# Forgetting attention on one core: the second group of transposed probabilities moves to the unit's own second PSUM bank

## The chip, the cores and the metric

The kernel runs on one core of a Trainium2 chip. The metric is the device time of one execution in microseconds (us). Three executions of the kernel before took 2426.31, 2428.12 and 2430.02 us; their median, 2428.12 us, is the time before.

## The reference

The reference is a two-layer trunk on a sequence of 1024 tokens of width 1024. Layer 0 mixes tokens with forgetting attention, layer 1 with a diagonal state-space mixer; each is followed by a SwiGLU block, and each of the four blocks has a norm before and after it. The change lies in the attention of layer 0, 16 heads of 64 columns:

```
for blk in range(seq_len // Q_BLOCK):          # 8 blocks of 128 queries
    s = einsum(qb, kb) * scale                 # against all keys up to the block's end
    s = s + c[q] - c[k]                        # sums of log forget gates
    s = where(q_pos >= k_pos, s, -inf)
    p = softmax(s)
    outs.append(einsum(p, vb))
o = concatenate(outs) * sigmoid(gate)
return o @ w_out
```

## The kernel before

Matrix products in full precision are made of two or three products of rounded parts: each operand is split into a high part, which ScalarE rounds to, and a low part, which VectorE gets by subtraction. So every operand that TensorE has made itself goes through a ScalarE copy and a VectorE subtraction that both read PSUM.

PSUM has eight banks of 512 float32 columns per partition, and the kernel holds all of it as one tile, `ps`, of which it hands out regions by hand. In the attention stage banks 0 and 1, and banks 2 and 3, are two slots of two banks for the scores, which alternate from unit to unit (`S`); banks 4 and 5 are for the projections (`PROJ`), bank 6 is for the transposes (`PTB`), bank 7 for the products with the values (`PVB`). Waits on PSUM are kept bank by bank.

`attend` runs over units, a unit being one head and one block of 128 queries; in each head the blocks go from 7 down to 0, and block `qb` sees `(qb + 1) * 128` keys. A unit passes three steps:

- `scores` (L542): TensorE makes the scores in the slot's banks (L551 and L552, one pair of matmuls for each 512 keys). Blocks 4 to 7 need both banks, blocks 0 to 3 the first alone. VectorE adds the bias in place and takes the row's minimum (L555). ScalarE writes the exponentials to SBUF, in `Pt`, with the row's sum (L561); `Pt` has two buffers. In the last two heads VectorE and GpSimd also divide by the sum (L563, L564).
- `transposes` (L576), one unit later: TensorE transposes the exponentials, 128 by 128, in groups of up to four which fill one bank (L588). ScalarE copies the group as the high part (L591), VectorE subtracts for the low part (L592). Blocks 4 to 7 have two groups, blocks 0 to 3 one; that makes 12 groups in a head, 192 in all.
- `values` (L594), for two units at a time, up to three units later: TensorE multiplies with the values in bank 7 (L607), and ScalarE and VectorE add the two halves into `o` (L611, L612).

Next to the attention of one pair of heads run the projections of the next pair and the gate of the pair before (`qkv`, `gate`; their matmuls are L272, L273, L274). `weave` writes the streams into one program in proportion to given weights, a chunk at a time (12 matmuls for a projection); the `yield` lines in `attend` tell it how much TensorE work has been written. The framework then places instructions on each engine's queue: it keeps the order of the program as a priority, and puts a later instruction first where, by its own times, an earlier one isn't ready. On the chip each engine's queue runs in the order so fixed. So projection matmuls stand between the transposes of one unit, at places that the planner chose. After the last head, the output projection (`out_proj`, L674) takes the scores' slots in the same turn.

The lines around the change:

```
units = [(h, qb) for h in range(NH) for qb in reversed(range(8))]
ps = self.S("S")                      # in scores: the slot of this unit
p2 = self.pb(PTB, (P, 4, P))          # in transposes: bank 6, for each group
nc.tensor.transpose(p2[:, i], p[:, (g + i) * P:(g + i + 1) * P], self.ident)
nc.scalar.copy(dh, p2[:, 0:n])
nc.vector.tensor_sub(dl, p2[:, 0:n], f32(dh))
```

Of the kernel before, what the change touches and what calls it, by code (L numbers as in the profile page):

```python
# [14 lines left out]
P = 128  # L15
# [16 lines left out]
PTB = (2,)  # L32
# [3 lines left out]
def f32(ap):  # L36
    return ap.bitcast(F32)
# [121 lines left out]
class Trunk:  # L159
# [369 lines left out]
    def attend(self, c, o):  # L529

        nc = self.nc
        units = [(h, qb) for h in range(NH) for qb in reversed(range(8))]
        An, pt, Pt, pv, rs, ri = {}, {}, {}, {}, {}, {}

        def load_bias(h):
            An[h] = self.R("An")
            nc.sync.dma_start(An[h], self.bcast(self.csum[h:h + 1, :], D))  # L540

        def scores(h, qb):  # L542
            qh, ql = c[h // 2]["q"][h % 2 * 2:h % 2 * 2 + 2]
            k = c[h // 2]["k"][h % 2]
            nk = (qb + 1) * P
            qs = slice(qb * P, nk)
            nc.gpsimd.tensor_add(An[h][:, qs], An[h][:, qs], self.cmask)  # L547
            ps = self.S("S")
            for c0 in range(0, nk, 512):
                c1 = min(c0 + 512, nk)  # L550
                nc.tensor.matmul(ps[:, c0:c1], qh[:, qs], k[:, c0:c1], start=True, stop=False)  # L551
                nc.tensor.matmul(ps[:, c0:c1], ql[:, qs], k[:, c0:c1], start=False, stop=True)  # L552
            with self.tc.high_priority(AHEAD):
                m = self.small("mx")
                nc.vector.tensor_tensor_reduce(out=ps[:, :nk], in0=ps[:, :nk], in1=An[h][:, :nk], op0=ALU.add, op1=ALU.min,  # L555
                                               scale=1.0, scalar=3e38, accum_out=m)
            p = Pt[h, qb] = self.R("Pt")
            if h // 2 not in rs:
                rs[h // 2] = self.small("rs", (P, 2, 8))
            r = rs[h // 2][:, h % 2, qb:qb + 1]  # L560
            nc.scalar.activation(p[:, :nk], ps[:, :nk], AF.Exp, bias=m, scale=-1.0, accum_out=r)  # L561
            if h >= NH - 2:
                nc.vector.reciprocal(r, r)  # L563
                nc.gpsimd.tensor_scalar(p[:, :nk], p[:, :nk], r, 1.0, op0=ALU.mult, op1=ALU.mult)  # L564

        def sums(hp):

            p2, r, x = self.pb(PTB, (P, P))[0:16], self.small("ri", (16, P)), self.R("RI")
            nc.tensor.transpose(p2, rs.pop(hp).rearrange("p a b -> p (a b)"), self.ident)
            nc.vector.reciprocal(r, p2)  # L570
            nc.sync.dma_start(self.ri_d[hp], r)
            for i in range(2):
                nc.sync.dma_start(x[i * 64:i * 64 + 64], self.bcast(self.ri_d[hp][i * 8:i * 8 + 8], D, 64))
            ri[hp] = x

        def transposes(h, qb):  # L576
            j, qq = qb // 2, qb % 2
            if qq:
                ng = (2 * j + 2 + 3) // 4
                pt[h, j] = [(self.R("pth", (P, 4, 256), F32R), self.R("ptl", (P, 4, 256), F32R)) for _ in range(ng)]  # L580
            p = Pt.pop((h, qb))
            for g in range(0, qb + 1, 4):
                n = min(4, qb + 1 - g)
                if g:
                    yield 0.11 * 4
                p2 = self.pb(PTB, (P, 4, P))
                for i in range(n):
                    nc.tensor.transpose(p2[:, i], p[:, (g + i) * P:(g + i + 1) * P], self.ident)  # L588
                th, tl = pt[h, j][g // 4]
                dh, dl = th[:, 0:n, qq * P:qq * P + P], tl[:, 0:n, qq * P:qq * P + P]  # L590
                nc.scalar.copy(dh, p2[:, 0:n])  # L591
                nc.vector.tensor_sub(dl, p2[:, 0:n], f32(dh))  # L592

        def values(h, j):  # L594
            h2, vt = h % 2, c[h // 2]["v"]
            if h2 == 0 and j == 3:
                o[h // 2] = self.R("o")
            r = slice(h2 * 64, h2 * 64 + 64)
            if j % 2:
                pv[h] = self.pb(PVB)  # L600
            out = pv[h][:, (j % 2) * 256:(j % 2) * 256 + 256]
            last = 2 * j + 1
            t = pt.pop((h, j))
            seq = [(0, 0)] + [(kb, i) for kb in range(1, last + 1) for i in (0, 1)] + [(0, 1)]
            for n, (kb, i) in enumerate(seq):
                lo = P if kb == last else 0
                nc.tensor.matmul(out[:, lo:], vt[kb // 4][:, kb % 4, h2, :], t[kb // 4][i][:, kb % 4, lo:],  # L607
                                 start=(n == 0), stop=(n == len(seq) - 1))
            if j % 2 == 0:
                d = o[h // 2][r, (j // 2) * 512:(j // 2) * 512 + 512]  # L610
                nc.scalar.copy(d, pv[h][64 - h2 * 64:128 - h2 * 64])  # L611
                nc.vector.tensor_add(d, d, pv[h][r])  # L612
                if h2 and j == 0 and h < NH - 2:
                    nc.gpsimd.tensor_mul(o[h // 2], o[h // 2], ri.pop(h // 2))

        load_bias(0)
        for i in range(len(units) + 3):
            hp = min(i, len(units) - 1) // 16
            if i < len(units):
                h, qb = units[i]  # L620
                if qb == 7:
                    yield 0.0, hp
                scores(h, qb)
                if qb == 2 and h + 1 < NH:
                    load_bias(h + 1)
                yield 0.16 * (qb + 1), hp
            if 1 <= i <= len(units):
                h, qb = units[i - 1]
                for x in transposes(h, qb):
                    yield x, hp  # L630
                yield 0.11 * (qb % 4 + 1), hp
                if h % 2 and qb == 0 and h < NH - 2:
                    sums(h // 2)
            if i >= 3 and (i - 3) % 2 == 1:
                h, qb = units[i - 3]
                values(h, qb // 2)
                yield 0.22 * (qb + 1), hp
# [1066 lines left out]
```

## Time and profile before

| what | before |
|---|---|
| median of three runs | 2428.12 us |
| profiled execution | 2426.33 us |
| its span | 2424.5 us |
| granted TensorE clock | 0.995 |
| TensorE matmul busy | 2359.3 us (97%) |
| VectorE busy | 1689.1 us (70%) |
| ScalarE busy | 1204.4 us (50%) |
| transposes, L588, attention stage | 576 matmuls, 100.2 us |
| ScalarE copies of them, L591 | 192, 92.0 us |
| VectorE subtractions, L592 | 192, 106.4 us |

The profile tells one execution. Its time is 1.8 us under the median. A busy time is the sum of an engine's records; matmuls are pipelined, and the end of a matmul's record is modelled, so that records overlap and a waiting TensorE loses more than the idle time between records. "PEld" is the load of weights, which runs under the matmuls. In rows of the timeline the first number is the start in us from the start of the span, the second the length; in brackets stands the engine's idle time before the row and what ended it. The attention stage lies between about 72 and 672 us.

### The profile page before, as it was taken

How to read it: one execution, taken by the hardware profiler on the slowest of the kernel's cores; microseconds unless marked ns; L12 is line 12 of the kernel's file. 1: busy time of each engine (PE TensorE's matmuls, PEld its weight loads, DVE VectorE, ACT ScalarE, POOL GpSimd, SP SyncE). 2: the span in 40 equal slices, each digit the busy share in tenths (PEclk: the TensorE clock that was granted, in tenths of full speed). 3: DMA queues.
4: the chain of work that ended last, by engine and by line, in shares of the span. 5: the costliest groups of instructions: out<-in, count | busy, mean ns of one | idle time of the engine just before them, and what ended most of it. 6: DMA issues, size and time to landing. Idle time of an engine off the chain costs nothing.

```text
span 2424.5 us, 31559 instructions
## 1 busy us (share of the span) xinstructions
PE 2359.3 (97%) x11683; PEld 1938.8 (80%) x11683; DVE 1689.1 (70%) x2684; ACT 1204.4 (50%) x2029; POOL 455.2 (19%) x427
## 2 busy tenths in 40 slices
PE   7999999999999999999999999999999999999997
PEld 5777778777777888888878779888878888888886
DVE  6867776677678967666668686763795656555867
ACT  6766676667646333434564563232453333333334
POOL 4222222222400034545520001410000000000003
PEclk9999999999999999999999999999999999999999
DMA  4121112121243444343688752443424333237874
GB/s 146 48 61 53 49 48 62 53 61 54 87 149 101 121 127 135 117 136 116 204 293 301 270 170 84 135 147 107 135 80 135 107 98 109 92 118 261 284 239 157
DMA packets 252427, 318.23 MB, mean 131 GB/s; under 512 B 34225, under 2 KB 179937, under 8 KB 252273
## 3 DMA queue, kind: packets, MB, share of 16 engines
q1 hardware_dynamic: 252272, 316.23, 40.9%
q8 instruction: 91, 1.49, 0.3%
q14 instruction: 64, 0.52, 0.1%
HBM read 238.46 MB, written 77.72 MB: 130 GB/s over the span
## 4 chain that ended last, share of the span: by engine, by line
PE 74%; DVE 12%; ACT 7%; DMA 3%; issue 3%; POOL 0%; SPq 0%; DVEq 0%; ACTq 0%; POOLq 0%
PE ps L841 33%; PE ps L943 10%; PE ps L272 7%; PE ps L274 7%; PE ps L273 7%; PE ps L588 2%; PE ps L607 2%; DVE ps L555 1%; DMA raw<-in_ffn_w_down_dram 1%; DMA rot_d<-ry 1%; ACT wh L253 1%; PE ps L552 1%; PE ps L551 1%; DVE ptl L592 1%; DVE y L318 1%
## 5 line engine op out<-in xcount | busy, mean ns | idle before, releaser
L841 PE MATMUL ps<-B,ah 128*128 128x512 f32 x1056 | 326.0, 390 | 0.3 <-ACT B L89 0.3
L943 PE MATMUL ps<-wdh,gh 128*128 128x512 f32 x616 | 241.4, 392 | 6.3 <-ACT m L962 3.7
L943 PE MATMUL ps<-wdh,gl 128*128 128x512 f32 x616 | 240.9, 391 | 1.9 <-DVE gl L254 1.9
L943 PE MATMUL ps<-wdl,gh 128*128 128x512 f32 x616 | 240.9, 391 | 0.8 <-DVE wdl L254 0.8
L841 PEld LDWEIGHTS ps<-B,ah 128*128 128x128 f32 x1056 | 198.1, 188 | 42.7 <-ACT B L89 1.2
L841 PE MATMUL ps<-ops,ah 128*128 128x512 f32 x704 | 218.2, 391 | 0.0
L272 PE MATMUL ps<-hT,wh 128*128 128x512 f32 x512 | 207.5, 406 | 1.3 <-DVE pt L429 0.7
L841 PE MATMUL ps<-B,al 128*128 128x512 f32 x528 | 205.4, 389 | 0.0
L273 PE MATMUL ps<-hT,wh 128*128 128x512 f32 x512 | 204.4, 399 | 0.0
L274 PE MATMUL ps<-hT,wl 128*128 128x512 f32 x512 | 202.6, 396 | 0.0
L253 ACT CAST gh<-gr 128x1024 fp32r<-128x1024 f32 (+1 forms) x78 | 81.1, 1040 | 166.4 <-PE ps L943 138.0
L592 DVE TENSOR_TENSOR ptl<-ps,pth 128x512 fp32r<-128x512 f32 x192 | 106.4, 554 | 78.6 <-ACT pth L591 73.6
L254 DVE TENSOR_TENSOR gl<-gr,gh 128x1024 fp32r<-128x1024 f32 (+1 forms) x78 | 98.3, 1262 | 84.0 <-ACT gh L253 83.7
L841 PEld LDWEIGHTS ps<-ops,ah 128*128 128x128 f32 x704 | 131.5, 188 | 28.7 <-issue 1.7
L812 DVE TENSOR_TENSOR al<-raw,ah 128x1024 fp32r<-128x1024 f32 x88 | 117.1, 1333 | 50.5 <-ACT ah L811 50.5
L1655 POOL TENSOR_TENSOR y<-m,s 128x512 f32<-128x512 f32 x4 | 6.5, 1628 | 764.3 <-DVE wdl L254 759.5
L547 POOL TENSOR_TENSOR An<-An,cmask 128x128 f32<-128x128 f32 x128 | 80.2, 629 | 365.8 <-DVE mx L555 332.3
L811 ACT CAST ah<-raw 128x1024 fp32r<-128x1024 f32 x88 | 92.6, 1052 | 101.8 <-PE ps L841 99.4
L943 PEld LDWEIGHTS ps<-wdh,gh 128*128 128x128 f32 x616 | 116.3, 189 | 32.8 <-ACT m L962 4.2
L943 PEld LDWEIGHTS ps<-wdh,gl 128*128 128x128 f32 x616 | 116.2, 189 | 26.9 <-DVE gl L254 2.7
L841 PE MATMUL ps<-ops,al 128*128 128x512 f32 x352 | 136.9, 389 | 0.0
L943 PEld LDWEIGHTS ps<-wdl,gh 128*128 128x128 f32 x616 | 116.3, 189 | 25.5 <-DVE wdl L254 1.5
(358 smaller groups left out, 5867.2 us busy)
## 6 DMA issues: line engine op xcount, KB each, us to landing
raw<-in_ffn_w_down_dram SPq DMA_DIRECT2D x98, 512.0 KB, 5.2
gr<-g_d SPq DMA_DIRECT2D x76, 512.0 KB, 4.4
raw<-in_ffn_w_gate_dram SPq DMA_DIRECT2D x44, 512.0 KB, 4.1
raw<-in_ffn_w_up_dram SPq DMA_DIRECT2D x44, 512.0 KB, 4.8
g_d<-s SPq DMA_DIRECT2D x66, 256.0 KB, 2.2
raw<-in_fox_w_in_dram SPq DMA_DIRECT2D x32, 512.0 KB, 4.3
g_d<-up SPq DMA_DIRECT2D x22, 512.0 KB, 2.7
g_d<-up SPq DMA_DIRECT2D x44, 256.0 KB, 2.9
```

Source lines behind the costliest of these rows:

```text
L253: self.nc.scalar.copy(h, src)
L254: self.lsub.tensor_sub(l, src, f32(h))
L272: mm(ps, lh, rh, start=start, stop=False)
L273: mm(ps, lh, rl, start=False, stop=False)
L274: mm(ps, ll, rh, start=False, stop=stop)
L547: nc.gpsimd.tensor_add(An[h][:, qs], An[h][:, qs], self.cmask)
L588: nc.tensor.transpose(p2[:, i], p[:, (g + i) * P:(g + i + 1) * P], self.ident)
L592: nc.vector.tensor_sub(dl, p2[:, 0:n], f32(dh))
L811: nc.scalar.copy(h, src)
L812: V.tensor_sub(l, src, f32(h))
L841: nc.tensor.matmul(bank, x[:, k], y, start=start and k == i == 0, stop=True, skip_group_check=True)
L943: nc.tensor.matmul(bank, x[:, j, t], y[:, j], start=start and i == 0, stop=True, skip_group_check=True)
```

## The change

For each unit `scores` notes the second bank of its slot, in `own`. `transposes` then chooses the bank of a group: the second group of blocks 4 to 7, and the one group of blocks 2 and 3, go to that second bank; the first group of blocks 4 to 7, and the groups of blocks 0 and 1, stay in bank 6. When a unit is transposed its scores have been read by the exponentials, so its slot is empty; the slot is next written by the scores of the unit after the next. Which instructions run, their sizes and their count stay as they are. The `yield` lines stay too.

```
-        An, pt, Pt, pv, rs, ri = {}, {}, {}, {}, {}, {}
+        An, pt, Pt, pv, rs, ri, own = {}, {}, {}, {}, {}, {}, {}
...
             ps = self.S("S")
+            own[h, qb] = self.slots[self.nS % len(self.slots)] + 1
...
-            p = Pt.pop((h, qb))
+            p, b = Pt.pop((h, qb)), own.pop((h, qb))
             for g in range(0, qb + 1, 4):
                 n = min(4, qb + 1 - g)
                 if g:
                     yield 0.11 * 4
-                p2 = self.pb(PTB, (P, 4, P))
+
+                p2 = self.bank(b, 1, (P, 4, P)) if g or qb in (2, 3) else self.pb(PTB, (P, 4, P))
```

## The prediction

> **What bounds the kernel now.** I read the page's busy shares first, then a table of stretches, then the waits of the attention stage, then the timelines of one head.
>
> ```profile
> PE 2359.3 (97%) x11683; PEld 1938.8 (80%) x11683; DVE 1689.1 (70%) x2684; ACT 1204.4 (50%) x2029; POOL 455.2 (19%) x427
> ...
> 72.00:672.00 600.00, 585.41 (x3163) 472.03 (x3164) 434.08 (x765) 415.02 (x792) 153.25 (x205) 1.00 0.20 59
> 600.00:672.00 72.00, 68.55 (x375) 53.31 (x374) 49.68 (x99) 48.72 (x90) 28.00 (x35) 1.00 0.35 106
> 672.00:760.00 88.00, 86.08 (x399) 69.25 (x399) 65.86 (x122) 46.00 (x94) 0.00 (x0) 1.00 0.43 137
> ```
>
> TensorE is the bound everywhere. The attention that the change touches runs from about 72 to 672 us; there TensorE is busy 585.4 of 600 us (the columns after the length are PE, weight loads, VectorE, ScalarE, GpSimd), at the full granted clock (1.00). The change removes no work, so it can only win back TensorE's stalls in that stage, and lose by new ones. Which stalls are there:
>
> ```profile
> PEld ps L588 <- DVE ptl L592: 39.9, 99, 1.1
> PE ps L588 <- DVE ptl L592: 8.5, 22, 0.6
> PEld ps L588 <- ACT Pt L561: 3.3, 6, 0.6
> PE ps L454 <- ACT pt L461: 0.9, 1, 0.9
> PE ps L588 <- POOL Pt L564: 0.8, 2, 0.4
> PE ps L588 <- ACT Pt L561: 0.6, 4, 0.2
> ```
>
> Each row is: who waited for whom, total us, times, longest. One wait stands out, the transposes of the probabilities (L588) for the VectorE subtraction (L592) that empties their single bank: 8.5 of about 14.6 us in which no matmul runs, and 39.9 us of idle before weight loads. Waits for the probabilities themselves (L561) are under a tenth of it.
>
> How such a wait comes about, in head 6, where the transposes of blocks 6 and 5 follow each other (TensorE, then ScalarE, then VectorE; start, length, instruction):
>
> ```profile
> 304.33 0.60 PE L588 MATMUL ps<-ident,Pt 128*128 128x128 f32 x4
> 304.68 0.48 PE L551 MATMUL ps<-p,p 128*128 128x512 f32 x1
> 305.00 0.39 PE L552 MATMUL ps<-p,p 128*128 128x512 f32 x1
> 305.22 0.28 PE L551 MATMUL ps<-p,p 128*128 128x256 f32 x1
> ...
> 308.19 0.60 PE L588 MATMUL ps<-ident,Pt 128*128 128x128 f32 x4
> ...
> 309.55 0.22 PE L551 MATMUL ps<-p,p 128*128 128x128 f32 x1
> ...
> 310.24 0.39 PE L274 MATMUL ps<-hT,wl 128*128 128x512 f32 x1
> 310.46 0.39 PE L272 MATMUL ps<-hT,wh 128*128 128x512 f32 x1
> 311.14 0.55 PE L588 MATMUL ps<-ident,Pt 128*128 128x128 f32 x3 [0.29 <-DVE ptl L592]
> 311.44 0.49 PE L273 MATMUL ps<-hT,wh 128*128 128x512 f32 x1
> 311.77 0.40 PE L274 MATMUL ps<-hT,wl 128*128 128x512 f32 x1
> 312.00 0.40 PE L272 MATMUL ps<-hT,wh 128*128 128x512 f32 x1
> ...
> 314.31 0.66 PE L588 MATMUL ps<-ident,Pt 128*128 128x128 f32 x4
> ```
>
> ```profile
> 307.30 0.91 ACT L561 ACTIVATE Pt<-ps,mx 128x768 f32<-128x768 f32 x1 [1.75 <-DVE mx L555]
> ...
> 309.13 0.59 ACT L591 CAST pth<-ps 128x512 fp32r<-128x512 f32 x1
> ```
>
> ```profile
> 306.19 0.96 DVE L555 CUSTOM_DVE_ANT_0 ps<-ps,An 128x768 f32<-128x768 f32 x1
> ...
> 310.40 0.68 DVE L592 TENSOR_TENSOR ptl<-ps,pth 128x512 fp32r<-128x512 f32 x1
> ```
>
> The first group of block 6 is transposed at 308.19, copied by ScalarE at 309.13 and subtracted by VectorE until 311.08; 0.06 us later the second group starts. So a group holds the bank 2.9 us here, and the second group, whose probabilities were ready long before, waited for nothing else. Block 5's exponential ended at 308.21 and its first transpose is at 314.31, 6.1 us later: the transposes run behind the exponentials, held by the bank. The placing puts projection matmuls into that time, but it expects the bank a little early, and then the whole in-order engine stands.
>
> **The change part by part.**
>
> *What is removed: the waits for the one bank.* A matmul of 512 columns starts 0.22 us after the one before (310.24 to 310.46) and its record lasts 0.39, so each shown idle hides about 0.16 us more: at 311.14 the engine lost 0.68 − 0.23 = 0.45 us where 0.29 is shown. The 22 shown waits thus cost 8.5 + 22 × 0.16 = 12.0 us. The other 77 of the 99 waiting weight loads cost between 0 and 0.16 each, 0 to 12.3; I take a third, 4. All bank waits: 16 us, with bounds 8.5 and 24.3, or 0.16 us per waiting group (16 / 99).
>
> Here a page bears on it. The Trainium skill, "Perfetto Trace Analysis", Identifying the Most-Contended Engine, holds that the busy share of matmuls misleads because they are pipelined, and that weight-load busy time tells more. By it the prize could be as large as the 39.9 us of load idle; the trace goes part of the way (0.45 lost where 0.29 shows), while most load idle lies under running matmuls.
>
> Per head there are 12 groups: two for each of blocks 7 to 4, one for each of 3 to 0. Afterwards the four second groups and those of blocks 3 and 2 use the scores' second banks; blocks 7 to 4 leave one group each in the old bank, a whole unit apart, and blocks 1 and 0 one each. The stage's 600 us hold 16 heads of 8 units, 4.7 us a unit, against 2.9 us for which a group held the bank. Only block 0 behind block 1 remains close, 1 group in 12. Removed: 16 × 11/12 = −14.7 us (bounds −7.8 and −22.3).
>
> *What is added: scores wait for the transposes' readers.* The next unit on the same slot is two units later. Only blocks 5 and 4 reach into a second bank that a second group (of blocks 7 and 6) has used: 2 per head, 32 waits. Blocks 3 to 0 stay in the first bank, and blocks 3 and 2 find the second bank two units after its last use; these cost nothing, covered by the units between. A waiting scores matmul holds everything behind it on TensorE, and VectorE's minimum and ScalarE's exponential of that block. In the rows above, block 4's second half went at 309.55, before block 6's second group at 311.14; now it must follow it and its evacuation. No row has this wait; the nearest is the same engine waiting for the same subtraction. Bounds: 0, where projection matmuls are placed between; and, where nothing lies between, the 2.9 us from a group's first transpose to the end of its subtraction, less its own 0.35 us on TensorE (304.33 to 304.68) and 0.54 us of first-half scores (304.68 to 305.22): 2.0 us a wait, 64 us in all. I take the mean of today's bank waits, 0.16 us, since the same placing fills in front of it with the same error: 32 × 0.16 = +5.1 us.
>
> *What takes the place of the bank: the probabilities.* With no bank to wait for, transposes follow their exponentials more closely. Bounds: 0, and all 112 first groups of blocks 7 to 1 at 0.16 us, 18 us. I take a quarter of them, 28 × 0.16 = +4.5 us, because the exponential of block 5 had 6.1 us in hand and a unit's scores, minimum (0.96 us) and exponential (0.91 us) fit into the unit before. ScalarE and VectorE get two copies (0.59 and 0.68 us) closer together; they are busy 415 and 434 of the stage's 600 us and take them in.
>
> *Adjacent groups.* A group inside a stream delays the next weight load: after 311.14 the L273 takes 0.33 us to the next start, not 0.23. Two groups back to back pay this 0.1 us once. 64 pairs: 0 to −6.4 us; half of them adjacent, since a projection chunk can lie between: −3.2 us.
>
> *The end of the stage.* Output-projection matmuls already run in the last head, in a scores' second bank:
>
> ```profile
> 652.24 0.40 PE L272 MATMUL ps<-woh,wh 128*128 128x512 f32 x1
> ...
> 656.16 0.39 PE L274 MATMUL ps<-woh,wl 128*128 128x512 f32 x1
> ...
> 658.63 0.63 PE L588 MATMUL ps<-ident,Pt 128*128 128x128 f32 x4
> ```
>
> Fifteen of them lie between these two ends, 3.5 us of cover at 0.23 each. Bank 3, where they go, will now be held until block 3 of the last head is transposed (658.63) and emptied. They are moved, not removed: +3.5 us if nothing else fills the gap. Against it, the last two heads run nearly one group after another, and the stretch 600 to 672 has 72 − 68.55 = 3.5 us of idle that a faster chain can take. I book 0, with both as bounds. No DMA and no instruction on GpSimd's or SyncE's queues is added or moved in the program.
>
> *Sum:* −14.7 + 5.1 + 4.5 − 3.2 + 0 = −8.3 us on the profiled execution's 2426.33 us (span 2424.5): 2418.0 us. The median of the runs, 2428.12, is 1.8 us above it: forecast 2419.8, rounded to 2420 us.
>
> **The rivals.**
>
> *A, the forecast (0.55):* stalls fall by about half, 2420 us; its own range, 2411 to 2423, is from half to twice the sum.
>
> *B, the waits only change their names (0.27):* the exponentials and the 32 scores waits take it all. With 11 us for the probabilities, between the 4.5 taken and the 18 of the bound, −14.7 + 5.1 + 11 − 3.2 = −1.8: 2426 us. For it: the same inexact placing stays. Against: exponentials now make only 3.9 us of load and matmul waits in 10.
>
> *C, slower: the second half of the scores of blocks 5 and 4 stands at the head of TensorE (0.13).* If it is placed directly behind the second group, each of the 32 waits costs 0.8 us, between 0.16 and 2.0: 25.6 us instead of 5.1, so 2420 + 20 = 2440 us; with half of them so, 2430. It decides from a mean of (14.7 + 3.2 − 4.5) / 32 = 0.42 us per wait. For it: block 4's scores now run 1.6 us ahead of the group they must follow. Against: today's bank waits have the same releaser and cost 0.16. The Trainium skill, "TensorE: Matmul & The Clock Gate", Part 3, What overlaps and what doesn't, says that matmuls start and end strictly in program order; by it nothing behind such a wait can slip past, as the trace agrees at 311.14, where an L273 that needed no bank stood behind the transposes.
>
> *D, more than forecast (0.05):* no new waits and all groups adjacent, −14.7 − 6.4 = −21.1: 2407 us; with the upper bound of the bank waits, 2399.
>
> **How the numbers follow.** A measurement of this kernel tells about 0.2%, 4.9 us, from no change: under 2423.3 is faster, over 2433.0 slower. A gives faster for 0.50 of its 0.55 and no change for the rest, B no change, C slower for 0.12 of its 0.13, D faster: faster 0.55, same 0.33, slower 0.12. The range leaves out D and most of C, under 0.2: 2410 to 2432 us.
>
> **What would show it.** In the profile after: TensorE's waits of the transposes for L592 fall from 8.5 us in 22 to under 3, and the load idle for it from 39.9 to under 15; runs of seven or eight transposes appear; a new row, scores matmuls (L551 and its load) for the subtraction, with at most 32 times and some 5 us; PE busy unchanged, and the stage's idle of 14.6 us near 10. C is shown by that new row at over 13 us; B by the transposes waiting for the exponentials at over 10 us. The forecast is wrong if the bank row stays, or if it goes and the time does not follow.

## The result and the profile after

The changed kernel took 2413.47 us (median of four runs, 2409.80 to 2415.58) against 2428.11 us for the kernel before beside it (2426.31 to 2430.02). The ratio is 0.9938, with a 95% interval of 0.9921 to 0.9955. Run once more on another occasion, it took 2415.27 us against 2426.49 us, a ratio of 0.9949 (0.9937 to 0.9961). So it is faster by 0.5 to 0.6%, 11 to 15 us, where −8.3 us and 2420 us were forecast.

The answers to the rows shown of before come from the page and the table of stretches (PE, weight loads, VectorE, ScalarE, GpSimd after the length):

```profile
PE 2350.9 (97%) x11683; PEld 1944.9 (81%) x11683; DVE 1687.5 (70%) x2684; ACT 1198.4 (50%) x2029; POOL 459.9 (19%) x427
...
72.00:672.00 600.00, 588.84 (x3229) 489.91 (x3230) 441.42 (x783) 418.67 (x811) 151.71 (x205) 1.00 0.21 64
```

Then come TensorE's waits in the same 600 us. The lines of the code have moved: L590 is the transposes (L588 before), L594 the subtraction that empties the bank (L592), L552 the scores (L551), L562 the exponential (L561):

```profile
PEld ps L552 <- DVE ptl L594: 9.2, 22, 0.7
...
PEld ps L590 <- DVE ptl L594: 6.9, 14, 0.8
PEld ps L590 <- POOL Pt L565: 6.8, 12, 1.8
...
PEld ps L590 <- ACT Pt L562: 3.6, 8, 1.3
...
PE ps L590 <- POOL Pt L565: 3.2, 6, 1.6
...
PE ps L590 <- DVE ptl L594: 2.8, 6, 0.6
...
PE ps L552 <- DVE ptl L594: 1.3, 6, 0.2
...
PE ps L590 <- ACT Pt L562: 0.9, 1, 0.9
```

The waits for bank 6 fell from 99 weight loads and 39.9 us to 14 and 6.9 us, and from 8.5 to 2.8 us between matmuls. The scores' new wait is there, 22 times. The waits for GpSimd (L565) occur in the last two heads only, which divide the probabilities there; between matmuls they grew from 0.8 us in 2 to 3.2 us in 6.

Head 6 again, on TensorE, in the same stretch of blocks 6, 5 and 4:

```profile
302.06 0.93 PE L590 MATMUL ps<-ident,Pt 128*128 128x128 f32 x7
...
305.05 0.33 PE L552 MATMUL ps<-p,p 128*128 128x128 f32 x1 [0.24 <-DVE ptl L594]
305.22 0.28 PE L553 MATMUL ps<-p,p 128*128 128x128 f32 x1
...
307.25 0.82 PE L590 MATMUL ps<-ident,Pt 128*128 128x128 f32 x6
...
311.13 0.27 PE L590 MATMUL ps<-ident,Pt 128*128 128x128 f32 x1
311.15 0.49 PE L609 MATMUL ps<-pth,vt 128*128 128x256 f32 x2
312.04 0.66 PE L590 MATMUL ps<-ident,Pt 128*128 128x128 f32 x4 [0.40 <-DVE ptl L594]
312.45 0.36 PE L609 MATMUL ps<-ptl,vt 128*128 128x256 f32 x1
```

Block 6 is transposed in one run of seven, block 5 in one of six. The second half of block 4's scores (305.05) waits for the evacuation, as foreseen, and stands 0.24 us. Of block 4 the single transpose of the second group (311.13) goes ahead of the four of the first (312.04), which still wait in bank 6 for block 5's.

**Where the time went.** The stage repeats itself with each pair of heads, so one period measures it. These are the first transposes of heads 6 and 8, before and after (the views end just behind the start, so that not every transpose of a group is counted in the row):

```profile
301.12 0.38 PE L588 MATMUL ps<-ident,Pt 128*128 128x128 f32 x2
...
378.63 0.38 PE L588 MATMUL ps<-ident,Pt 128*128 128x128 f32 x2
```

```profile
294.89 0.38 PE L590 MATMUL ps<-ident,Pt 128*128 128x128 f32 x2
...
370.31 0.38 PE L590 MATMUL ps<-ident,Pt 128*128 128x128 f32 x2
```

A pair took 77.51 us and takes 75.42, so 2.09 us less. The five pairs from head 2 to head 12 gain 2.07 to 2.14 us each, the first 1.8 and the seventh 3.0. At the first transpose of head 14 (609.60 us before, 594.10 after) the changed kernel is 15.5 us ahead. The next stage begins with the first gate-and-up matmul (L841 before, L843 after; the times behind the comma are the first and the last start):

```profile
L841 PE MATMUL ps<-B,ah x1056: 389/389/505, 757.7 to 2194.9; 128*128 128x512 f32 x176
```

```profile
L843 PE MATMUL ps<-B,ah x1056: 387/389/504, 741.5 to 2180.4; 128*128 128x512 f32 x176
```

There the changed kernel is 16.2 us ahead, so that the last two heads and the output projection add 0.7. At the end of the spans, 2424.5 and 2411.7 us, it is 12.8 us ahead. So 3.4 us of this execution's gain are lost later. In the gate-and-up stage TensorE waits for GpSimd's work on the next layer's parameters, which it hardly did before:

```profile
PEld ps L1221 <- POOL s5w L1207: 3.0, 4, 1.0
PE ps L1221 <- POOL s5w L1207: 1.9, 4, 0.7
```

Over these four waits, at 923, 1004, 1085 and 1166 us, the lead falls in steps to 12.2 us; what follows gives a little of it back.

### The profile page after: what moved, and what is told of

Same layout as the page of the kernel before. It is cut to its first block, busy times and chain, and to the rows that moved or that the text cites. A ratio compares the mean times of both kernels' runs of the same rounds, so it can differ in the third digit from the quotient of the medians.

```text
span 2411.7 us, 31471 instructions
## 1 busy us (share of the span) xinstructions
PE 2350.9 (97%) x11683; PEld 1944.9 (81%) x11683; DVE 1687.5 (70%) x2684; ACT 1198.4 (50%) x2029; POOL 459.9 (19%) x427
## 4 chain that ended last, share of the span: by engine, by line
PE 72%; DVE 12%; ACT 5%; issue 4%; DMA 3%; POOL 3%; SPq 0%; DVEq 0%; ACTq 0%; POOLq 0%
PE ps L843 29%; PE ps L945 11%; PE ps L272 7%; PE ps L273 7%; PE ps L274 7%; PE ps L609 2%; PE ps L590 2%; PE ps L552 1%; DVE ps L556 1%; DMA raw<-in_ffn_w_down_dram 1%; POOL s5w L1207 1%; PE ps L553 1%; DMA rot_d<-ry 1%; DVE y L318 1%; ACT y L295 1%
## 5 line engine op out<-in xcount | busy, mean ns | idle before, releaser
L843 PE MATMUL ps<-B,ah 128*128 128x512 f32 x1056 | 326.0, 390 | 0.3 <-ACT B L89 0.3
L843 PEld LDWEIGHTS ps<-B,ah 128*128 128x128 f32 x1056 | 198.1, 188 | 42.7 <-ACT B L89 1.2
L843 PE MATMUL ps<-ops,ah 128*128 128x512 f32 x704 | 218.3, 391 | 0.0
L272 PE MATMUL ps<-hT,wh 128*128 128x512 f32 x512 | 204.6, 400 | 1.2 <-DVE pt L429 0.7
L843 PE MATMUL ps<-B,al 128*128 128x512 f32 x528 | 205.4, 389 | 0.0
L273 PE MATMUL ps<-hT,wh 128*128 128x512 f32 x512 | 201.4, 393 | 0.0
L843 PEld LDWEIGHTS ps<-ops,ah 128*128 128x128 f32 x704 | 131.3, 188 | 28.7 <-issue 1.7
L594 DVE TENSOR_TENSOR ptl<-ps,pth 128x512 fp32r<-128x512 f32 x192 | 102.5, 551 | 56.5 <-ACT pth L593 56.1
L843 PE MATMUL ps<-ops,al 128*128 128x512 f32 x352 | 137.0, 389 | 0.0
```

Of the source, the lines that this page charges most:

```text
L272: mm(ps, lh, rh, start=start, stop=False)
L273: mm(ps, lh, rl, start=False, stop=False)
L843: nc.tensor.matmul(bank, x[:, k], y, start=start and k == i == 0, stop=True, skip_group_check=True)
```

## The experiments

Each is an edit of the changed kernel, timed beside the kernel before. "Stage" is the start of the first gate-and-up matmul in the profiled execution (757.7 us before, 741.5 changed).

| run | median, us | ratio to before, 95% | stage, us |
|---|---|---|---|
| e1 second groups only | 2410.49 | 0.9926 (0.9913 to 0.9938) | 743.5 |
| e2 blocks 3 and 2 only | 2425.50 | 0.9987 (0.9979 to 0.9996) | 754.9 |
| e3 blocks 1 and 0 too | 2411.64 | 0.9930 (0.9917 to 0.9944) | 743.6 |
| e4 groups swapped | 2410.43 | 0.9925 (0.9912 to 0.9937) | 743.0 |
| e5 groups adjacent | 2411.20 | 0.9933 (0.9919 to 0.9947) | 739.1 |
| e6 groups kept apart | 2420.73 | 0.9972 (0.9962 to 0.9982) | 750.3 |
| e7 last two heads as before | 2409.77 | 0.9937 (0.9923 to 0.9951) | 743.2 |
| e8 first groups in the first bank | 2412.19 | 0.9939 (0.9926 to 0.9952) | 745.1 |
| e9 e6 and block 4 moved | 2417.23 | 0.9960 (0.9945 to 0.9974) | 745.4 |
| e10 block 4 moved | 2408.57 | 0.9935 (0.9922 to 0.9948) | 741.4 |
| e11 e5 and block 4 moved | 2408.68 | 0.9923 (0.9911 to 0.9935) | 739.7 |
| e12 changed kernel again | 2415.27 | 0.9949 (0.9937 to 0.9961) | 741.7 |

The two profiles of the changed kernel agree on the stage within 0.2 us (741.5 and 741.7), while its nine runs range from 2409.80 to 2417.53. So, as far as two executions can tell, the stage's mark resolves what the totals do not.

Some costs below are "counted from start to start": the time from each matmul's start to the next one's, less what the same pair takes in these traces when nothing waits (0.227 us behind a matmul of 512 columns, 0.109 from one transpose to the next), put down to the wait that the profile names there. The count runs from the first transpose of head 0 to the stage's mark. It holds what a waiting TensorE loses under its records too.

**Which groups carry the gain (e1, e2, e3).** The edits change the choice of the bank alone:

```
-  if g or qb in (2, 3)
+  if g                   # e1
+  if qb in (2, 3)        # e2
+  if g or qb < 4         # e3
```

> Only the second groups of blocks 7 to 4 go to the scores' second bank; blocks 3 and 2 stay in bank 6. Theory (the gain is the second group's wait for the bank that the first one holds): nearly all of the gain stays, 2412 to 2416 us, and the transposes' waits for the subtraction stay under 12 us. Rival (the bank is relieved by every group taken away, each alike: 64 of the 96 moved groups are moved here): two thirds of the 14.6 us, about 2418 us.

> Only the groups of blocks 3 and 2 go to the second bank; both groups of blocks 7 to 4 stay in bank 6. Theory: those groups waited for under 1 us in all before, so 2426 to 2429 us. Rival (each group taken away alike, 32 of 96): a third of the gain, about 2423 us.

> As the changed kernel, and the groups of blocks 1 and 0 go to the second bank too, so that bank 6 holds the first groups of blocks 7 to 4 alone. Theory: only block 0 behind block 1 still met a held bank, 16 groups at about 0.1 us: 0 to -2 us against the changed kernel, 2411 to 2414 us. Rival (the gain grows with each group that leaves bank 6): -3 us or more, under 2411 us.

The second groups alone give 14.2 of the 16.2 us at the stage's mark (e1; its total, 2410.49 us, is even below the changed kernel's and below what the theory expected). Blocks 3 and 2 alone give 2.8 us at the mark and 2.6 in the total, less than the third that the rival had, though more than the theory's none; TensorE's waits for the bank stay. In e2 they are:

```profile
PEld ps L590 <- DVE ptl L594: 35.9, 84, 1.0
...
PE ps L590 <- DVE ptl L594: 8.5, 21, 0.8
```

Taking blocks 1 and 0 away as well (e3) gains nothing. Its waits for bank 6 between matmuls stay (2.7 us in 6), the scores wait more often for a second bank (37 weight loads, 14.3 us, where the changed kernel has 22 and 9.2), and the mark comes 2.1 us later. So it isn't how many groups leave the bank that counts most, but that a unit's second group no longer waits for its first.

**What the scores' new wait costs (e4, e8).**

```
-  p2 = self.bank(b, 1, ...) if g or qb in (2, 3) else self.pb(PTB, ...)
+  p2 = self.bank(b, 1, ...) if g == 0 and qb > 1 else self.pb(PTB, ...)       # e4
+  p2 = (self.bank(b - 1 + (g > 0), 1, ...) if qb > 3 else                     # e8
+        self.bank(b, 1, ...) if qb > 1 else self.pb(PTB, ...))
```

> As the changed kernel, but of blocks 7 to 4 the first group goes to the second bank and the second group to bank 6, so that the scores of blocks 5 and 4 wait for the evacuation of a first group, which is made about 0.5 us earlier, and no longer for that of a second. Theory (the new wait of the scores costs little, about 5 us): the scores' waits for the subtraction fall, the next unit's first group gains a wait for nobody, and the time is 0 to -4 us against the changed kernel, 2409 to 2414 us. Rival (the new wait costs 10 us or more): 2408 us or less.

> As the changed kernel, but the first groups of blocks 7 to 4 also leave bank 6, for the first bank of their own scores' slot: the scores of blocks 5 to 2 then wait for an evacuation before their first half. This doubles and moves forward the new wait: 96 waits where there were 32. Theory (a scores wait costs about 0.3 us, as the profile of the changed kernel has it): +8 to +20 us against the changed kernel, 2421 to 2433 us. Rival (the order is made around the wait and it costs nothing): within 3 us of it.

In e4 the scores wait for the earlier of the two evacuations. They wait 10 times instead of 22, and the time is 2410.43 us, as the theory had it; the mark comes 1.5 us later, and more of the transposes wait for bank 6 (19 weight loads, 14 in the changed kernel):

```profile
PEld ps L590 <- DVE ptl L594: 10.8, 19, 0.8
...
PEld ps L552 <- DVE ptl L594: 5.4, 10, 0.6
```

Of e8 the theory expected 2421 us or more, and was wrong; it took 2412.19. Its waits:

```profile
PEld ps L552 <- DVE ptl L594: 16.5, 44, 0.8
...
PEld ps L590 <- DVE ptl L594: 2.0, 6, 0.4
PE ps L552 <- DVE ptl L594: 1.8, 8, 0.3
```

Twice as many scores wait (44 against 22) and for 16.5 us against 9.2 in weight loads, but only 1.8 us of it fall between matmuls. Much of the rest lies under running matmuls. The stage is 3.6 us longer, the total no different. The 3.6 us are not the price of the 22 more waits alone, since e8 also removes waits for bank 6 (6.9 to 2.0 us in weight loads) and lets the transposes wait longer for the exponentials. Counted from start to start, the 44 waits cost 7.1 us and the 22 of the changed kernel 3.9: 0.16 and 0.18 us each, as the forecast took it. A price of 0.8 us is out: rival C is excluded.

**Adjacent groups (e5, e6, e9).** e5 moves the share of work between the groups behind them; e6 moves the next scores' share and the share after the second group between them, so that projection matmuls are written there.

```
                 if g:
-                    yield 0.11 * 4
+                    yield 0.0            # e5, and + 0.44 behind the second group
+                    yield 0.11 * 4 + w   # e6, w: shares of the scores and of the second group
```

> As the changed kernel, but the two groups of a unit stand directly behind each other in the program: the share of work between them (0.44) is counted after the second. In the order for TensorE 53 groups of the 192 then follow another without a matmul between, 47 in the changed kernel, and none in the kernel before. Theory (fewer changes between transposes and other matmuls are part of the gain, about 0.1 us for each): -1 us or less to be seen, 2411 to 2415 us. Rival (adjacency harms, since two evacuations then meet): slower by 3 us or more.

> As the changed kernel, with the same banks, but the share of the next unit's scores and that behind the second group are counted between the two groups of blocks 7 to 4, so that projection matmuls are written between them: 13 groups follow another without a matmul between, 47 in the changed kernel. Theory A (removed waits for the bank are most of the gain): at 0.1 us a change 3 to 4 us are lost, 2415 to 2419 us. Rival B (adjacency is most of the gain): 10 us or more are lost, 2423 us or more.

e5's stage is 2.4 us shorter than the changed kernel's (739.1 against 741.5); the ratios of the totals, 0.9933 and 0.9938, do not part them. Fewer changes between transposes and other matmuls are not what shortens it: counted from start to start, the waits for bank 6 fall from 5.6 to 1.5 us and the scores' from 3.9 to 2.1, while the waits for the exponentials grow from 1.9 to 5.6. e6 lost more than half of the gain, between the two expectations: 8.8 us in the stage. But it is not the distance of the groups that did most of this. One wait per pair of heads has grown in it. VectorE and TensorE of e6, in head 8:

```profile
387.42 2.55 DVE L522 TENSOR_TENSOR pt<-o,pt 128x1024 f32<-128x1024 f32 x1 [1.55 <-POOL o L616]
389.87 0.72 DVE L556 CUSTOM_DVE_ANT_0 ps<-ps,An 128x512 f32<-128x512 f32 x1
...
390.47 0.71 DVE L594 TENSOR_TENSOR ptl<-ps,pth 128x512 fp32r<-128x512 f32 x1
```

```profile
391.24 0.66 PE L590 MATMUL ps<-ident,Pt 128*128 128x128 f32 x4 [1.24 <-DVE ptl L594]
392.66 0.27 PE L590 MATMUL ps<-ident,Pt 128*128 128x128 f32 x1
```

The gate's multiplication (L522) takes 2.5 us of VectorE, the subtraction of block 5's first group stands behind it, and block 4's first group finds bank 6 held. In the changed kernel the same wait is 0.40 us (312.04, in head 6). Among the waits of e6's stage it is this row, six times in the stage:

```profile
PE ps L590 <- DVE ptl L594: 7.7, 6, 1.5
```

e9 takes this one wait away from e6, by other means than distance:

```
-  p2 = self.bank(b, 1, ...) if g or qb in (2, 3) else self.pb(PTB, ...)
+  p2 = self.bank(b - (qb == 4 and g == 0), 1, ...) if g or qb in (2, 3, 4) else self.pb(PTB, ...)
```

> The kernel whose two groups are kept apart (e6), with one more move: the first group of block 4 leaves bank 6 for the first bank of its own slot. In e6 that group waited once per pair of heads, some 1.4 us each, behind the subtraction of block 5's first group, which stood behind the gate's multiplication on VectorE. Theory (e6 lost through that one wait more than through its 13 instead of 47 adjacent groups): 6 us or more come back, 2412 to 2415 us. Rival (keeping the groups apart is what e6 lost by): 2419 us or more.

The first transposes of heads 6 and 8 in e6, then in e9:

```profile
297.72 0.38 PE L590 MATMUL ps<-ident,Pt 128*128 128x128 f32 x2
...
374.65 0.49 PE L590 MATMUL ps<-ident,Pt 128*128 128x128 f32 x3
```

```profile
295.27 0.49 PE L590 MATMUL ps<-ident,Pt 128*128 128x128 f32 x3
...
371.04 0.38 PE L590 MATMUL ps<-ident,Pt 128*128 128x128 f32 x2
```

A pair takes 76.93 us in e6, 75.77 in e9 and 75.42 in the changed kernel. So of the 1.51 us per pair that e6 lost, 1.16 come back with that one move. But the move gains something in the changed kernel too, 0.30 us (75.12, e10 below), so 0.86 of e6's loss is the longer wait. The other 0.65 us are seen when e9 is held against e10, which has the same banks and 34 more adjacent groups. They aren't the price of that many changes between transposes and other matmuls, which is next to nothing (last section). In e9 more transposes wait for their exponentials: counted from start to start, 28 waits of 8.0 us, where e10 has 14 of 4.6. The total of e9 doesn't show this cleanly: its runs spread from 2411.98 to 2422.01 us, and the profiled one lost time well after the stage. Its median, 2417.23 us, lies between both expectations, so the split of e6's loss rests on the periods.

**The end of the stage (e7).** Heads 14 and 15 keep the old banks:

```
-  if g or qb in (2, 3)
+  if h < 14 and (g or qb in (2, 3))
```

> As the changed kernel for heads 0 to 13, as the kernel before for heads 14 and 15, which have little other work beside them. Theory (the gain arises evenly in the first 14 heads, 2 us per pair, and the faster chain of the last two is given back to the output projection): 2413 to 2417 us. Rival (the end of the stage, where transposes ran one group after another, carries a third or more): 2418 us or more.

2409.77 us, below what either side expected: the last two heads give nothing that the total shows, 1.7 us in the stage, of which 1.4 are there at the first transpose of head 14 (595.47 us against 594.10).

**A better version (e10, e11, e12).** e10 is the changed kernel with e9's line, e11 is e5 with it, e12 the changed kernel unaltered.

> The changed kernel with the first group of block 4 in the first bank of its own slot. Theory (of the changed kernel's waits for bank 6 this group's, 0.6 us for each of 7 pairs, is the only one left of size): -2 to -4 us against the changed kernel of the same call. Rival (the placing only moves the wait to the scores of block 2): within 1 us of it.

> Both steps at once: no share of work between the two groups (as e5) and block 4's first group in the first bank of its own slot; 60 groups follow another without a matmul between. Theory: the best so far, -4 to -6 us against the changed kernel of the same call. Rival: the same as it within 2 us.

> The changed kernel once more, unaltered, to stand beside the three others on the same chip. Theory and rival: 2410 to 2416 us. If it lies at 2410 us, the 2 to 3 us by which most other variants lay under its first measurement are the measurement's.

From the first transpose of head 6 to that of head 8 e10 takes 75.12 us (294.54 to 369.66) and e11 74.90 (293.76 to 368.66), against 75.42. In e10 the waits of the transposes for bank 6 fall from 2.8 us to none between matmuls, but those for the exponentials grow from 0.9 to 2.5, and those for GpSimd's division in the last two heads from 3.2 to 5.0:

```profile
PE ps L590 <- POOL Pt L565: 5.0, 9, 1.7
...
PE ps L590 <- ACT Pt L562: 2.5, 7, 0.9
```

So what is removed passes in good part to the next causes: at the stage's mark e10 (741.4 us) is level with the changed kernel, and e11 (739.7) is 2.0 us ahead of it but not ahead of e5 (739.1). By the mark both come out as their rivals had it, though not by the rival's wait in e10: the scores wait as before (22 weight loads, 9.1 us). In the total both gain more than their theories expected, 6.7 and 6.6 us. The total of e11, 2408.68 us with a ratio of 0.9923 (0.9911 to 0.9935), lies below the changed kernel's beside it, 0.9949 (0.9937 to 0.9961), by 0.27%. That doesn't make it the best version: the ratios of e1 (0.9926) and e4 (0.9925) are as low, and the stage accounts for only 2.0 of the 6.6 us. e10's 2408.57 us has an interval that meets the changed kernel's; the totals do not part them. Nor did the changed kernel come out at 2410 us the second time, so what most variants have over it in the total isn't explained by its first measurement. The profiles show where it arises: e10 and the unaltered kernel (e12) pass the mark within 0.3 us of each other and end 3.4 us apart, at 2406.7 and 2410.1 us.

## Why the prediction was right

Direction and mechanism held, and the likeliest case A was what came. The sizes held less well: at the end of the attention stage the gain was 16.2 us, nearly twice the forecast's 8.3, and what was lost behind the stage brought the total back to 11 to 15 us. That part of the agreement is luck. By its steps, counted from start to start:

- *Waits for the one bank, −14.7 us.* The 99 waiting groups cost 23.7 us before, 0.24 each, where the forecast reckoned 16 us and 0.16; its bound, 24.3, was near; the 39.9 us of idle before weight loads were not the prize. The weight loads counted at a third of 0.16 us cost more, and a group that waited also starts its second transpose about 0.05 us late: the three at 311.14 take 0.30 us to the next start, where three that don't wait take about 0.25 (four take 0.35, 304.33 to 304.68). After the change 14 waits of 5.6 us are left, so −18.1. The second groups were the place (e1). What I had wrong is which wait would cost most: five of the 14 are block 0's behind block 1's, all under running matmuls, but the six that also stop the matmuls are those of block 4's first group behind block 5's. There the gate's work delays the evacuation, the multiplication on VectorE and, in the changed kernel, loads of function tables on ScalarE (head 8, ScalarE):

```profile
384.81 1.28 ACT L521 ACT_TABLE_LOAD   x1
386.10 0.59 ACT L593 CAST pth<-ps 128x512 fp32r<-128x512 f32 x1
```

A quarter of the old cost stayed where a twelfth was expected; that the price of a wait was taken too low hid this in the sum.

- *Scores wait, +5.1 us.* After: 22 of the 32 possible waits, 3.9 us. The mechanism and the price of one were right, their number was smaller. Rival C fell.
- *The probabilities, +4.5 us.* This term was mis-sized, and what came of it came elsewhere. The transposes' waits for ScalarE's exponentials went from 2.1 us to 1.9, so about 0. The 6.1 us between block 5's exponential and its transposes in head 6 did not vanish with the bank's wait; the program writes the next block's scores before a block's transposes, and in head 8 they are still 4.5 us apart (ScalarE, then TensorE):

```profile
377.28 0.90 ACT L562 ACTIVATE Pt<-ps,mx 128x768 f32<-128x768 f32 x1 [2.54 <-DVE mx L556]
```

```profile
382.65 0.82 PE L590 MATMUL ps<-ident,Pt 128*128 128x128 f32 x6
```

In the last two heads, where GpSimd divides the probabilities, the transposes do wait for them: 5.7 us instead of 1.4. The forecast did not name this wait.

- *Adjacent groups, −3.2 us.* This term was wrong. 47 groups became adjacent, but the 0.1 us that a matmul behind a group loses was already made up by the group (last section), and the saving is at most 0.4 us.
- *The end of the stage, 0.* From head 14's first transpose to the mark −0.7 us: the 4.4 us more of waiting for GpSimd are outweighed by other waits that shrank.

In the seven pairs up to head 14, −16.9 us for the bank, +3.7 for the scores and −0.1 for the exponentials make −13.3 of the −15.4 us by which they became shorter. Half of the rest is a wait of the projections for ScalarE (L272 for L412, 1.0 us) that is gone, the other half I could not assign to one wait. The forecast's −8.3 thus missed mainly by the 4.5 us for the probabilities and by the low price of a bank wait, and the adjacent groups' −3.2 made up for part of that. Rival B fell with the probabilities, and D's shape (−21) was not reached, since a quarter of the old waits stayed and the scores do wait.

Of what was to show each step, the bank's rows came under both marks (2.8 and 6.9 us), runs of six to eight transposes appeared, and the idle of the 600 us fell to 11.2. The new row stayed under 33 times, but with 9.2 us in weight loads and 1.3 between matmuls it was twice the 5 us expected, still under the 13 that were to show C. TensorE's busy time was not unchanged: it fell by 8.4 us. From the first transpose to the stage's mark the idle between records fell by only 4.8 us (16.3 to 11.5) of the 16.1 won; most of the loss had lain under records.

The 3.4 us lost behind the stage were not foreseen. Waits for GpSimd's work in the gate-and-up stage (L1221 in the changed kernel), 1.4 to 2.0 us between matmuls, stand in both profiles of the changed kernel and in those of e5, e6 and e9; in the other nine, before among them, there are none. From the mark to the end of the span those five take 1668.4 to 1674.8 us, the nine 1662.8 to 1666.9. GpSimd runs the same instructions in the same order behind the mark in all of them; what decides whether the waits occur was not tried and stays open.

## What to carry to other kernels

Where two pieces of one unit share a buffer, look at the wait between the pieces, not at the buffer's load: the four second groups of a head carried 14.2 of the 16.2 us, and relieving the same bank of two other tenants gave 2.8. A region that is free by the order of the program costs little to borrow when its next writer has other work placed before it; here 22 new waits cost about 4 us, and 22 more another 3. An experiment that shifts the order of a planned program can bring a wait of its own, which has to be taken out before the experiment says anything; and the version without it has to be held against one that has the same move.

## What the hardware showed that was not expected

In two executions of the changed kernel on different occasions the start of the next stage agrees within 0.2 us (741.5 and 741.7 us), while the totals of these two differ by 1.5 us and those of all nine by 7.7. In these two, then, the difference arises behind the attention.

And changing from transposes to projection matmuls costs next to nothing, though one row alone says otherwise. The first projection matmul behind a run takes 0.32 us to the next start instead of 0.23, whether seven transposes went before (head 5) or four (head 6), in the changed kernel:

```profile
261.11 0.93 PE L590 MATMUL ps<-ident,Pt 128*128 128x128 f32 x7
261.79 0.48 PE L272 MATMUL ps<-hT,wh 128*128 128x512 f32 x1
262.11 0.39 PE L273 MATMUL ps<-hT,wh 128*128 128x512 f32 x1
...
294.89 0.60 PE L590 MATMUL ps<-ident,Pt 128*128 128x128 f32 x4
295.24 0.48 PE L272 MATMUL ps<-hT,wh 128*128 128x512 f32 x1
295.56 0.40 PE L273 MATMUL ps<-hT,wh 128*128 128x512 f32 x1
295.79 0.40 PE L274 MATMUL ps<-hT,wl 128*128 128x512 f32 x1
```

From the first transpose to the second matmul behind it the seven take 1.00 us (261.11 to 262.11) and the four 0.67 (294.89 to 295.56). Three transposes more are thus 0.33 us, 0.11 each. Four of these and one matmul of 0.23 make 0.67 already, so no price of the change is left. The last transpose of a run gives way early, by as much as the matmul behind it is late.
